# Moving every SBUF tile that TensorE reads to a multiple of 512 bytes

## Chip, cores and metric

One NeuronCore of a Trainium2 chip runs the whole layer as one launch. The metric is the device time of that launch in microseconds (us). The sections on the profile speak of PE (TensorE's matmuls), PEld (its weight loads), DVE (VectorE), ACT (ScalarE), POOL (GpSimd) and SP (the queue that issues nearly all DMAs). In a matmul the *stationary* operand (the weights) is loaded into the array ahead of it, and the *moving* operand is streamed through; both are read from SBUF. SBUF is addressed here in bytes per partition, and "at 352" means 352 bytes past a multiple of 512.

## What is computed

One layer of a hybrid backbone: 1024 latent tokens of width 1024 and 256 context tokens, all fp32.

```
mod = silu(c) @ w_mod + b_mod            # six shift/scale/gate vectors; context has its own
h   = modulate(rms_norm(x), sh1, sc1)    # hc the same for the context
q, k, v, g, f = split(h @ w_in)          # k, v of the context give the first states
y = (sig_r * (ret(q,k,v) readout * silu(g)) @ w_ret_out      # bidirectional retention
   + sig_f * fft2_mix(f) @ w_four_out) @ w_out               # gates: sigmoid(h @ w_bg + b)
x = x + g1 * y
u = conv3(modulate(rms_norm(x), sh2, sc2) @ w_up)            # 2 x 2816 wide
x = x + g2 * (gelu(u_a) * u_v) @ w_down
return rms_norm(x)
```

## The kernel before

Nearly every product is made with three matmuls: each fp32 operand is split into a rounded high part and a remainder (`split`, L96 to L98: ACT casts the high part, DVE subtracts for the low part), both in the type float32r, and hi*hi, hi*lo and lo*hi are summed in PSUM. Three helpers issue them, each in that order of three: `mm3` (L114 to L117; all projections), `chain` (L771 to L775; the up projection) and `step` (L1014 to L1018; the down projection). The up and the down projection use a fast matrix product with seven products of half the size in place of eight.

Counted from the loops, there are 5,268 float32r matmuls with 512 moving columns: 2,496 by `mm3` (the first k/q/v pass `pk` 192, gates `g` 384, `gr` 384 and `gf` 384, Fourier input `f` 192 and output `fo` 192, retention output `re` 384, output projection `wo` 384), 1,848 by `chain` (L774) and 924 by `step` (L1017). Another 1,440 have 256 columns (the context projections `kc` and `vc`, the later `qk` and `v`). The retention itself, the transposes and the small Fourier products are in plain fp32, two passes each, most with 128 columns.

The stages follow each other in the code: norm and first projection (to about 75 us), retention with the projections of the next head pair between its steps (to 550), branch gates and Fourier branch (to 700), retention output and output projection (to 890), transposes and operands of the FFN (to 985), up projection (to 1360), down projection and final norm. The order of instructions on each engine is fixed when the program is built; a planner with estimated durations makes it, so that other work may stand between the matmuls of one loop.

SBUF is filled from both ends. Pools opened with `side="right"` (`wp`, L65: the weights of the projections as `hi`, `lo` and the raw loads; later `fw`: the operands of the up projection) are laid out down from the right end, all others up from the left. A tile's place follows from the sizes of those before it, each rounded up to 32 bytes. The first tile, `ident`, begins at byte 16,512 and the right end is byte 229,344. The pool `const` (L63) holds `ident`, `silrow`, the small vectors and `ones`; after it stand the big tiles of `ap` (the activations `h` hi and lo, later operands of the FFN), then the pool of the stage (`sp` L244, `rp` L353, `zp` and `fp` L597, `bp` and so on). With the sizes in the code:

- all big tiles on the left lie at 352, all on the right at 480, because 229,344 is 480 past a multiple of 512 and the sizes there are multiples of 512;
- in `rp`, the tables `dec` (128 bytes), `lg`, `expc`, `sm` and `smx` stand between bigger tiles, so that the tiles after them (`tab`, `pt`, `on`, `vc`, `kcfb`) lie at 64, while `qT`, `kT`, `kfb`, `qfb`, `ss`, the values and `s0_all` lie at 352;
- in `zp`, `cdft` (516 bytes) and `x64` (80 bytes) push what follows (`wfo`, `X`, `F`) to 480, while `z` and `fourc` lie at 352;
- in the down projection (pool `dp`, L1003) both operands, `oa` and `ob` (and `first`), are on the left at 352.

So `step` has both operands at the same place within 512 bytes, and every other float32r matmul has one operand at 352 and one at 480.

Of the kernel before, what the change touches and what calls it, by code (L numbers as in the profile page):

```python
# [8 lines left out]
F32 = mybir.dt.float32  # L9
# [7 lines left out]
P = 128  # L17
D = 1024
L = 1024
LC = 256  # L20
KD = D // P
# [22 lines left out]
def tile_block(ctx: ExitStack, tc: tile.TileContext, a: dict, out: bass.AP):  # L44
    nc = tc.nc
    V, S, T, G = nc.vector, nc.scalar, nc.tensor, nc.gpsimd
    dma = nc.sync.dma_start

    def tt(out, in0, in1, op):
        V.tensor_tensor(out=out, in0=in0, in1=in1, op=op)  # L50

    def tsc(out, in0, s1, op0, s2=None, op1=None):
        if op1 is None:
            V.tensor_scalar(out=out, in0=in0, scalar1=s1, scalar2=None, op0=op0)
        else:
            V.tensor_scalar(out=out, in0=in0, scalar1=s1, scalar2=s2, op0=op0, op1=op1)
# [3 lines left out]

    ADD, SUB, MUL = ALU.add, ALU.subtract, ALU.mult

    const = ctx.enter_context(tc.tile_pool(name="const", bufs=1))  # L63
    wps = ctx.enter_context(ExitStack())
    wp = wps.enter_context(tc.tile_pool(name="wp", bufs=2, side="right"))  # L65
    ops = ctx.enter_context(ExitStack())
# [17 lines left out]
    mhalf = const.tile([P, 4], F32, name="mhalf")  # L84
    epsc = const.tile([P, 1], F32, name="epsc")
    ycx = silrow[:, :LC]
    ones = const.tile([P, 256], F32, name="ones")
    V.memset(mhalf, -0.5)
    V.memset(epsc, EPS)

# [5 lines left out]
    def split(hi, lo, src):  # L96
        S.copy(hi, src)  # L97
        tt(lo, src, hi.bitcast(F32), SUB)  # L98
# [15 lines left out]
    def mm3(o, l, r, first, last):  # L114
        T.matmul(o, l[0], r[0], start=first, stop=False)  # L115
        T.matmul(o, l[0], r[1], start=False, stop=False)  # L116
        T.matmul(o, l[1], r[0], start=False, stop=last)  # L117
# [4 lines left out]
    def pick(w, *idx):  # L122
        return tuple(t[idx] for t in w)
# [3 lines left out]
    def blk(i, n=P):  # L127
        return slice(i * n, i * n + n)
# [12 lines left out]
    def half():  # L141
        if not halves:
            for i in (0, 1):
                ps = rt(f"half{i}")
                halves.extend((ps[:, :256], ps[:, 256:]))
        halves.append(halves.pop(0))
        return halves[-1]
# [44 lines left out]
    def t2(pool, name, n=512, dt=F32, tag="t2"):  # L192
        return pool.tile([P, 512], dt, tag=tag, bufs=T2[tag], name=name)[:, :n]
# [12 lines left out]
            stt(t1, t1, c, tr, ADD, MUL)  # L206
        stt(dst, t1, 1.0, ti.bitcast(F32), ADD, MUL)

    def rstd_bc(pool, slices, n, name, y=None):
        ps = half()  # L210
        for k in range(KD):
            sq = t2(pool, f"sq{name}{k}", n)
            q = 32 * (k % 4)
            S.activation(sq, slices[k], AF.Square)
            T.matmul(ps[q:q + 32, :n], ones[:, 0:32], sq, start=(k < 4), stop=(k >= 4), tile_position=(0, q))
        part = t2(pool, f"pt{name}", n)
        S.copy(part, ps[:, :n])
        T.matmul(ps[:, :n], ones[:, 128:256], part, start=True, stop=True)
        if y is None:
            y = pool.tile([P, n], F32, name=f"y{name}")  # L220
        u, v = (t2(pool, f"{c}{name}", n) for c in "uv")
        S.activation(y, ps[:, :n], AF.Abs_reciprocal_sqrt, bias=epsc, scale=1.0 / D)
        tsc(v, ps[:, :n], 1.0 / D, MUL, EPS, ADD)
        tt(u, y, y, MUL)
        tt(u, u, v, MUL)
        tsc(u, u, -0.5, MUL, 1.5, ADD)
        tt(y, y, u, MUL)
        return y
# [15 lines left out]
    with tc.tile_pool(name="sp", bufs=1) as sp:  # L244
        xh = [sp.tile([P, KD, 512], F32, name=f"xh{t}") for t in range(2)]
        ccs = sp.tile([P, KD, 2], F32, name="ccs")
        sil = sp.tile([P, KD, 32], F32, name="sil")
        V.memset(sil, 0.0)
        dma(ccs, a["cc"])
        S.activation(sil[:, :, 0:2], ccs, AF.Silu)  # L250
        V.memset(ones[:, 0:128], 1.0)
        V.memset(ones[:, 128:256], 1.0 / 32)
        w0 = [None] * KD

        groups = [(g // 2, blk(g % 2, 256), (2 * g, 2 * g + 1)) for g in range(4)]

        def load_x(g):
            t, c, _ = groups[g]
            for q in range(2):
                dma(xh[t][:, blk(q, 4), c], a["xT"][2 * g + q].rearrange("p (k n) -> p k n", k=4))  # L260

        def x_slices(g):
            t, c, _ = groups[g]
            return [xh[t][:, k, c] for k in range(KD)]

        w0t = [tuple(wp.tile([P, 4, 512], F32R, tag=f"w{n}", name=f"w0{i}{n}") for n in ("hi", "lo")) for i in range(2)]

        def load_w0(q):
            raw = wp.tile([P, 1024], F32, tag="wraw", bufs=3, name=f"w0r{q}")
            dma(raw, a["w_qkv0"][q // 2, q % 2])  # L270
            raw = raw.rearrange("p (k n) -> p k n", k=2)
            for k in range(2):
                w0[2 * q + k] = pick(w0t[q // 2], ALL, 2 * (q % 2) + k)
            ks = slice(2 * (q % 2), 2 * (q % 2) + 2)
            split(w0t[q // 2][0][:, ks], w0t[q // 2][1][:, ks], raw)

        def k_step(k, n, ps):
            mm3(ps, pick(hT[n // 4], ALL, k, blk(n % 4)), w0[k], k == 0, k == KD - 1)

        def h_step(g, k):  # L280
            t, c, _ = groups[g]
            h_slice(xh[t][:, k, c], ys[g], hT[t][0][:, k, c], hT[t][1][:, k, c], k, 0, ONACT[g])

        def k_steps(g, k):
            for n in groups[g][2]:
                k_step(k, n, psk[n])

        def mod(k):
            if k < KD:
                mod_cols(sp, sil, a["wm1"], k)  # L290
                if k % 2 == 0:
                    load_w0(k // 2)

        def rms(g):
            c = groups[g][1]
            return rstd_bc(sp, x_slices(g), c.stop - c.start, f"x{g}")

        psk = [kp.tile([P, 512], F32, name=f"pk{n}") for n in range(6)]
        load_x(0)
        for t, n in ((bmodc, "bmodc"), (norms, "norms"), (sel, "sel")):  # L300
            dma(t, a[n])
        ys = [rms(0)]
        mod(0)
        h_step(0, 0)
        k_steps(0, 0)
        load_x(1)
        ys.append(rms(1))
        mod(1)
        h_step(1, 0)
        k_steps(1, 0)  # L310
        for g in range(2):
            h_step(g, 1)
            k_steps(g, 1)
        load_x(2)
        mod(2)
        ys.append(rms(2))
        h_step(2, 0)
        for g in range(2):
            h_step(g, 2)
            k_steps(g, 2)  # L320
        k_steps(2, 0)
        h_step(2, 1)
        mod(3)
        for k in range(1, KD):
            mod(k + 3)
            if k + 2 < KD:
                h_step(0, k + 2)
                h_step(1, k + 2)
            if k + 1 < KD:
                h_step(2, k + 1)  # L330
            if k == 3:
                load_x(3)
                ys.append(rms(3))
            if k == 4:
                cs = [sp.tile([P, 4, 256], F32, tag="mraw", bufs=8, name=f"cs{i}") for i in range(2)]
                for i in range(2):
                    dma(cs[i], a["ctxT"][:, 4 * i:4 * i + 4, :])
                rstd_bc(sp, [cs[k // 4][:, k % 4, :] for k in range(KD)], LC, "c", ycx)
            if k > 2:
                k_steps(0, k)  # L340
                k_steps(1, k)
            if k >= 4:
                h_step(3, k - 4)
            k_steps(2, k)
        for k in range(KD - 4, KD):
            h_step(3, k)
        psk += [rt(f"pk{n}") for n in (6, 7)]
        for k in range(KD):
            k_steps(3, k)
        wg0 = wload_k(a["w_g"], 0, "wg")  # L350

    T2 = {"t2": 3, "t2b": 3}
    with tc.tile_pool(name="rp", bufs=1) as rp:  # L353
# [4 lines left out]
        hc = [tuple(t4(f"hc{i}{n}", dt=F32R) for n in "hl") for i in range(2)]  # L358
        kcs = t4("kcs", (2, 512))
        s0_all = rp.tile([P, H, P], F32, name="s0_all")  # L360
        dec = rp.tile([P, 32], F32, name="dec")
        lg = rp.tile([P, 32], F32, name="lg")
        expc = rp.tile([P, 6], F32, name="expc")
        ropec = rp.tile([P, NT, 2, 32], F32, name="ropec")
        decm = rp.tile([P, 4, P], F32, name="decm")
        sm = rp.tile([P, 56], F32, name="sm")
        smx = rp.tile([P, 56], F32, name="smx")
        for t, n in ((ropec, "ropec"), (dec, "dec"), (expc, "expc"), (decm, "decm")):
            dma(t, a[n])
        for i in range(2):  # L370
# [148 lines left out]
        for n in range(NT):  # L519
            ps = psk[n].rearrange("p (n c) -> p n c", n=1)  # L520
            t, c = n // 4, slice(n % 4, n % 4 + 1)
# [7 lines left out]
        cs = [ctt[k // 4][:, k % 4, :] for k in range(KD)]  # L529
# [267 lines left out]
    with tc.tile_pool(name="mp", bufs=2, reuse_waits="tile") as mp:  # L797
# [59 lines left out]
        for t in range(2):  # L857
            y = tuple(big(ap if t == 0 else bp, f"y{t}{n}") for n in "hl")
# [50 lines left out]
    with tc.tile_pool(name="ff", bufs=1, reuse_waits="tile") as ff:  # L909
# [76 lines left out]
        for n, i in enumerate(order):  # L986
            cs = up_mm(i)
# [15 lines left out]
    with tc.tile_pool(name="dp", bufs=1, reuse_waits="tile") as dp:  # L1003
# [28 lines left out]
        c = [[dp.tile([P, 512], F32, name=f"c{q}{n}") for n in N4] for q in range(3)]  # L1032
# [202 lines left out]
```

## Time and profile before

| | |
|---|---|
| time, median of 3 runs | 1594.49 us (1592.68 to 1598.33) |
| the profiled execution: its own time | 1593.61 us |
| the profiled execution: span of its instructions | 1591.8 us |
| PE busy, share of the span | 1536.5 us, 97% |
| PEld | 1275.2 us, 80% |
| DVE | 1032.2 us, 65% |
| ACT | 630.0 us, 40% |
| mean granted TensorE clock | 0.986 of full speed |

The busy time of PE is the union of its matmuls, whose ends overlap the starts of the next. A matmul that lasts 390 ns therefore doesn't take 390 ns of the span: what it takes is the distance from its start to the next start. That distance is read from the chain of work that ended last, where consecutive matmuls of one tile are merged into one piece with its length and count, or from the start times in the timeline.

### The profile page before, as it was taken

What the parts mean: (1) busy time and instruction counts of PE and PEld (TensorE: products, weight loads), DVE (VectorE), ACT (ScalarE), POOL (GpSimd) and SP (SyncE); (2) the same over time, 40 slices, a digit from 0 to 9 for tenths busy, and PEclk for the clock granted to TensorE, in tenths of its full rate; (3) what the DMA queues carried; (4) which work ended last, traced back from release to release, by engine and by line L of the source; (5) the groups of instructions that cost most, each with busy time, mean ns of one, the idle gap of its engine ahead of it and who ended that gap; (6) DMA issues with size and microseconds to landing.
All of it is one profiled execution on the core that took longest, in us unless ns stands there. A gap on an engine that the chain in (4) does not pass through costs nothing.

```text
span 1591.8 us, 20417 instructions
## 1 busy us (share of the span) xinstructions
PE 1536.5 (97%) x7806; PEld 1275.2 (80%) x7806; DVE 1032.2 (65%) x1920; ACT 630.0 (40%) x1084; POOL 70.6 (4%) x115
## 2 busy tenths in 40 slices
PE   6999999999999999999999879999999999799996
PEld 3789989898878888888888658888888888678885
DVE  5586848467562552135566688878788787596668
ACT  6554132231322231122354545445445444344443
POOL 0000000000000000000000000110000001000001
PEclk9999999999999999999999889999999999899998
DMA  9235122214442411237385322332222222783324
GB/s 356 98 123 183 60 69 85 73 61 132 128 154 97 154 49 67 80 131 265 120 278 172 120 94 85 120 106 99 99 100 99 99 100 106 270 318 100 94 92 179
DMA packets 76482, 207.45 MB, mean 130 GB/s; under 512 B 9616, under 2 KB 13984, under 8 KB 76384
## 3 DMA queue, kind: packets, MB, share of 16 engines
q1 hardware_dynamic: 70224, 185.96, 34.9%
q0 software_dynamic: 6160, 20.19, 3.4%
q8 instruction: 61, 1.00, 0.3%
q14 instruction: 37, 0.30, 0.1%
HBM read 162.82 MB, written 43.26 MB: 129 GB/s over the span
## 4 chain that ended last, share of the span: by engine, by line
PE 84%; DVE 8%; DMA 5%; ACT 1%; issue 1%; SPq 0%; POOL 0%; DVEq 0%; ACTq 0%; POOLq 0%
PE x L774 16%; PE y L774 8%; PE dx L1017 7%; PE z L774 4%; DMA mt<-wmT 3%; PE dy L1017 2%; PE dz L1017 2%; PE wo L116 2%; PE wo L115 2%; PE gf L115 2%; PE re L117 2%; PE re L115 2%; PE wo L117 2%; PE g L117 2%; PE re L116 2%; PE gf L117 2%
## 5 line engine op out<-in xcount | busy, mean ns | idle before, releaser
L774 PE MATMUL x<-s,wt 128*128 128x512 f32 x528 | 133.0, 397 | 10.1 <-ACT wt L97 10.1
L774 PEld LDWEIGHTS x<-s,wt 128*128 128x128 f32 x528 | 100.0, 190 | 34.3 <-ACT wt L97 10.3
L1017 PE MATMUL dx<-ob,oa 128*128 128x512 f32 x480 | 112.5, 396 | 8.3 <-DVE ob L50 4.8
L1017 PEld LDWEIGHTS dx<-ob,oa 128*128 128x128 f32 x480 | 91.5, 191 | 28.6 <-DVE ob L50 5.5
L50 DVE TENSOR_TENSOR wt<-t,wt 128x512 fp32r<-128x512 f32 x88 | 59.9, 686 | 47.5 <-ACT wt L97 40.0
L179 DVE SCALAR_TENSOR_TENSOR mt<-mt,silrow 128x512 f32<-128x512 f32 x64 | 41.7, 689 | 67.1 <-DMA mt<-wmT 67.1
L50 DVE TENSOR_TENSOR oa<-pr,oa 128x512 fp32r<-128x512 f32 x73 | 50.2, 690 | 52.8 <-ACT oa L97 52.8
L97 ACT CAST oa<-pr 128x512 fp32r<-128x512 f32 x73 | 45.2, 622 | 96.1 <-PE dx L1017 54.2
L774 PE MATMUL x<-a,wb 128*128 128x512 f32 x264 | 67.7, 403 | 2.9 <-DVE acc L50 2.0
L97 ACT CAST wt<-t 128x512 fp32r<-128x512 f32 x88 | 54.4, 623 | 39.3 <-PE x L774 25.6
L774 PE MATMUL z<-a,wb 128*128 128x512 f32 x264 | 70.0, 399 | 0.0
L774 PE MATMUL y<-s,wt 128*128 128x512 f32 x264 | 67.1, 397 | 0.0
L774 PE MATMUL y<-s,wb 128*128 128x512 f32 x264 | 65.2, 395 | 0.0
L774 PE MATMUL x<-a,wt 128*128 128x512 f32 x264 | 65.0, 395 | 0.0
L774 PEld LDWEIGHTS x<-a,wb 128*128 128x128 f32 x264 | 50.9, 194 | 15.8 <-ACT wb L97 3.8
L59 DVE SCALAR_TENSOR_TENSOR t<-ca,convw,t 128x1023 f32<-128x1023 f32 x44 | 56.2, 1278 | 9.6 <-ACT t L952 9.4
L1017 PE MATMUL dy<-ob,oa 128*128 128x512 f32 x264 | 60.8, 390 | 1.2 <-ACT oa L97 1.2
L495 ACT ACTIVATE on<-o,nm,rst 128x128 f32<-128x128 f32 x64 | 24.0, 455 | 94.0 <-DVE nm L59 94.0
L774 PEld LDWEIGHTS z<-a,wb 128*128 128x128 f32 x264 | 50.1, 190 | 11.7 <-ACT wb L97 0.2
L774 PEld LDWEIGHTS y<-s,wt 128*128 128x128 f32 x264 | 50.0, 189 | 11.6
L1017 PEld LDWEIGHTS dy<-ob,oa 128*128 128x128 f32 x264 | 49.4, 188 | 12.1 <-ACT oa L97 1.6
L774 PEld LDWEIGHTS y<-s,wb 128*128 128x128 f32 x264 | 49.7, 188 | 11.6
(946 smaller groups left out, 4096.7 us busy)
## 6 DMA issues: line engine op xcount, KB each, us to landing
pr<-p_d SPq DMA_DIRECT2D x73, 256.0 KB, 2.6
mt<-wmT SPq DMA_DIRECT2D x32, 512.0 KB, 3.9
p_d<-t POOLq DMA_DIRECT2D x44, 256.0 KB, 2.6
d<-w_down SPq DMA_DIRECT2D x44, 256.0 KB, 5.4
p_d<-s POOLq DMA_DIRECT2D x33, 256.0 KB, 3.1
xh<-xT SPq DMA_DIRECT2D x8, 512.0 KB, 7.2
r_d<-rr SPq DMA_DIRECT2D x16, 256.0 KB, 4.0
sr_d<-sr SPq DMA_DIRECT2D x8, 512.0 KB, 4.8
```

The lines of the kernel that those rows point to most:

```text
L50: V.tensor_tensor(out=out, in0=in0, in1=in1, op=op)
L59: V.scalar_tensor_tensor(out=out, in0=in0, scalar=s, in1=in1, op0=op0, op1=op1)
L97: S.copy(hi, src)
L115: T.matmul(o, l[0], r[0], start=first, stop=False)
L116: T.matmul(o, l[0], r[1], start=False, stop=False)
L117: T.matmul(o, l[1], r[0], start=False, stop=last)
L179: V.scalar_tensor_tensor(out=raw[:, c], in0=raw[:, c], scalar=1.0, in1=silrow[:, c], op0=MUL, op1=MUL, accum_out=acc[:, h:h + 1])
L495: S.activation(on[:, n, :], o[:, blk(n)], AF.Identity, bias=nm[:, n:n + 1], scale=rs[:, n:n + 1])
L774: T.matmul(ps, x[:, l, k], y[:, r, k], start=(first and k == 0 and l + r == 0), stop=(k == 3 and l == 1), skip_group_check=True)
L1017: T.matmul(ps[n], x[l][:, blk(n)], y[r], start=(first and l + r == 0), stop=(l == 1), skip_group_check=True)
```

## The change

Two tiles that nothing reads are added and filled with zeros: `edge`, 480 bytes at the right end, and `base`, 40 fp32 words (160 bytes) at the left end of `const`. `ones` moves from `const` to the pool `sp` of the first stage and is handed to `rstd_bc` as an argument. In `rp`, five small tables become slices of one tile `small` of 1,024 bytes. Worked out with the sizes, the left tiles then start at 23,552 (a multiple of 512) and the right end is 228,864 (another one). `wfo`, `X` and `F` come to lie at 128, 128 bytes past `z` as before. The tiles of the first stage behind `ccs` (64 bytes) come to lie at 64. No other instruction is added or taken out.

```diff
+    edge = ctx.enter_context(tc.tile_pool(name="edge", bufs=1, side="right"))
+    V.memset(edge.tile([P, 120], F32, name="edge"), 0.0)
     const = ctx.enter_context(tc.tile_pool(name="const", bufs=1))
+    V.memset(const.tile([P, 40], F32, name="base"), 0.0)
...
-    ones = const.tile([P, 256], F32, name="ones")
...
-    def rstd_bc(pool, slices, n, name, y=None):
+    def rstd_bc(pool, ones, slices, n, name, y=None):
...
         sil = sp.tile([P, KD, 32], F32, name="sil")
+        ones = sp.tile([P, 256], F32, name="ones")
...
         s0_all = rp.tile([P, H, P], F32, name="s0_all")
-        dec = rp.tile([P, 32], F32, name="dec")
-        lg = rp.tile([P, 32], F32, name="lg")
-        expc = rp.tile([P, 6], F32, name="expc")
+        small = rp.tile([P, 2, 128], F32, name="small")
+        dec, lg, expc = small[:, 0, 0:32], small[:, 0, 32:64], small[:, 0, 64:70]
         ropec = rp.tile([P, NT, 2, 32], F32, name="ropec")
         decm = rp.tile([P, 4, P], F32, name="decm")
-        sm = rp.tile([P, 56], F32, name="sm")
-        smx = rp.tile([P, 56], F32, name="smx")
+        sm, smx = small[:, 1, 0:56], small[:, 1, 64:120]
```

## Rows read from the trace of the kernel before

**Rows 1.** The page: busy share of each engine, busy tenths and granted clock by slice.

```profile
PE 1536.5 (97%) x7806; PEld 1275.2 (80%) x7806; DVE 1032.2 (65%) x1920; ACT 630.0 (40%) x1084; POOL 70.6 (4%) x115
...
PEclk9999999999999999999999889999999999899998
```

**Rows 2.** Busy time by stage: stretch, its length, each engine's busy us, clock.

```profile
75.00:550.00 475.00, 471.98 (x3060) 422.65 (x3059) 288.32 (x749) 146.90 (x258) 17.31 (x16) 1.00 0.33 108
...
640.00:800.00 160.00, 160.00 (x690) 129.69 (x690) 63.02 (x71) 42.41 (x52) 0.55 (x1) 1.00 0.46 155
...
890.00:985.00 95.00, 81.90 (x337) 65.40 (x338) 73.85 (x121) 51.36 (x90) 2.79 (x3) 0.88 0.30 98
985.00:1360.00 375.00, 375.00 (x1616) 304.11 (x1615) 303.69 (x397) 178.28 (x264) 37.69 (x70) 1.00 0.31 105
```

**Rows 3.** PE's longest waits: who waited for whom, total us, times, longest.

```profile
PE x L774 <- ACT wt L97: 10.1, 1, 10.1
PE half L215 <- ACT sqx L214: 6.2, 1, 6.2
```

**Rows 4.** Chain that ended last, up projection: start, length in us, piece and count.

```profile
1014.84 5.57 PE x L774 x24
...
1065.03 5.58 PE x L774 x24
```

**Rows 5.** The same chain in the down projection.

```profile
1487.85 29.92 PE dx L1017 x132
1517.77 29.92 PE dz L1017 x132
```

**Rows 6.** Timeline of PE, first fo matmul and the gf after 24 of them.

```profile
642.85 0.39 PE L115 MATMUL fo<-zh,wfo0hi 128*128 128x512 f32 x1
...
648.44 0.40 PE L115 MATMUL gf<-h0h,wbf6hi 128*128 128x512 f32 x1
```

**Rows 7.** The chain from 700 us: its longest single matmuls, in order of time.

```profile
713.43 0.24 PE fo L115
715.05 0.24 PE fo L116
716.68 0.24 PE re L117
718.31 0.24 PE re L115
719.93 0.24 PE re L116
```

**Rows 8.** Timeline of PE, 256 columns: two stretches, first and last row of each.

```profile
109.08 0.28 PE L115 MATMUL kc<-wkc0hi,hc0h 128*128 128x256 f32 x1
...
111.96 0.28 PE L115 MATMUL kc<-wkc0hi,hc0h 128*128 128x256 f32 x1
...
186.03 0.28 PE L115 MATMUL v<-wv1hi,h0h 128*128 128x256 f32 x1
...
187.10 0.28 PE L115 MATMUL v<-wv1hi,h0h 128*128 128x256 f32 x1
```

**Rows 9.** Timeline of PE, plain fp32 in two passes with 256 columns, and what follows.

```profile
565.69 1.02 PE L656 MATMUL zc<-fourc,X 128*128 128x256 f32 x4
566.55 0.38 PE L659 MATMUL zc<-fourc,X 128*128 128x128 f32 x2
```

**Rows 10.** The chain at 153 us: plain fp32 with 128 columns.

```profile
153.64 1.79 PE kv L455 x16
```

**Rows 11.** The page, costliest groups: instruction, count, busy us, mean ns of one.

```profile
L50 DVE TENSOR_TENSOR wt<-t,wt 128x512 fp32r<-128x512 f32 x88 | 59.9, 686 | 47.5 <-ACT wt L97 40.0
...
L50 DVE TENSOR_TENSOR oa<-pr,oa 128x512 fp32r<-128x512 f32 x73 | 50.2, 690 | 52.8 <-ACT oa L97 52.8
```

**Rows 12.** Timelines at the start and of the small tables: DVE, PE and SP's queue.

```profile
1.17 0.17 DVE L251 MEMSET ones<- 128x128 f32 x1
...
6.23 2.30 PE L215 MATMUL half<-sqx,ones 128*32 128x256 f32 x9 [6.23 <-ACT sqx L214]
...
77.91 0.91 SPq L371 DMA_DIRECT2D ctt<-ctxT  x2
...
97.37 0.42 DVE L50 TENSOR_TENSOR hc1l<-ctt,hc1h 128x256 fp32r<-128x256 f32 x1
...
110.76 0.28 PE L117 MATMUL kc<-wkc0hi,hc1l 128*128 128x256 f32 x1
```

**Rows 13.** Tiles dec and expc: time from a DMA's issue to its landing.

```profile
DMA to landing us min/median/max: 2.4/2.4/2.4
...
DMA to landing us min/median/max: 2.7/2.7/2.7
```

More of the change, by code (lines that the diff above doesn't have):

```diff
@@ L295, in rms @@
             c = groups[g][1]
-            return rstd_bc(sp, x_slices(g), c.stop - c.start, f"x{g}")
+            return rstd_bc(sp, ones, x_slices(g), c.stop - c.start, f"x{g}")
         psk = [kp.tile([P, 512], F32, name=f"pk{n}") for n in range(6)]
@@ L337, in tile_block @@
                     dma(cs[i], a["ctxT"][:, 4 * i:4 * i + 4, :])
-                rstd_bc(sp, [cs[k // 4][:, k % 4, :] for k in range(KD)], LC, "c", ycx)
+                rstd_bc(sp, ones, [cs[k // 4][:, k % 4, :] for k in range(KD)], LC, "c", ycx)
             if k > 2:
```

## Prediction

> **What bounds the kernel now.** I read the page first: PE is busy for 97% of the span at a granted clock of 0.9 or more in nearly every slice [rows 1]. The table by stage says where that holds without a gap: from 75 to 550 us, from 640 to 800 and from 985 to 1360 PE is busy for all or nearly all of the stretch at clock 1.00, which is the upper level, 2.4 GHz, while DVE has room (304 of 375 us in the up projection, its fullest stage). Only around 890 to 985 does something else set the pace [rows 2]. PE's longest wait of the whole run is 10.1 us [rows 3]. So the time is the number of matmuls times the distance between their starts, and a change of that distance shows nearly whole in the result. That makes the distance the thing to read.
>
> At 2.4 GHz and one column per cycle, 512 columns take 512 / 2.4 = 213.3 ns. No float32r matmul here reaches that. In the up projection 24 take 5.57 or 5.58 us, 232.3 ns each [rows 4]; in the down projection 132 take 29.92 us, 226.7 ns each, in two stretches alike [rows 5]. Same shape, same type, same clock, and the order hi*hi, hi*lo, lo*hi is the same; the difference of 5.7 ns is 2.4%.
>
> What differs is where the operands lie. In the down projection both lie at 352; in the up projection one is at 352 on the left and one at 480 on the right of SBUF. Distance alone isn't it: `fo` reads `z` and `wfo`, both on the left and within 60 KB of each other, one at 352 and one at 480, and 24 of its matmuls take 648.44 - 642.85 = 5.59 us, 232.9 ns each [rows 6]. Nor does it matter which operand is at 480: the first pass and `wo` have the moving one there, the other loops the stationary one, and the longest single matmuls return alike in `fo` and `re`, every 1.63 us, which is every seventh matmul [rows 7]. They take 0.24 us, the rest less. Such a beat is what two interleaved reads make that get into each other's way at a changing moment: the moving columns of one matmul and the weights of the next. Where the places agree there is no beat, only a steady 13.3 ns over the 213.3.
>
> **The change part by part.**
>
> *Places.* After it, both operands of every float32r matmul lie at 0 but for `fo`, whose weights stay 128 bytes off their moving operand. So the relation that only `step` has now holds for all 512-column matmuls but 924 that have it already and 192 of `fo`: 5,268 - 924 - 192 = 4,152. If they come to the 226.7 ns of rows 5, that is 4,152 x (232.4 - 226.7) = 23.7 us less. The trace shows no float32r matmul at a multiple of 512, so whether the absolute place counts too has to be bounded: at worst nothing is gained by it (226.7), at best the steady 13.3 ns goes as well. The nearest row for the best is plain fp32 with 256 columns in two passes, the same 512 array cycles, at 352: four in 0.86 us, 215 ns each [rows 9]. So the array can follow at 215; I take 226.7, since it is measured with this type and differs by nothing but the absolute place, and keep 215 for the range.
>
> *256 columns.* These 1,440 need 106.7 ns at the same rate, and take 2.88 us / 24 = 120.0 ns in one stretch and 1.07 us / 9 = 118.9 in another, at the same places [rows 8]. None has both operands at one place. The nearest row is the steady excess of rows 5, 13.3 ns per matmul, which gives 120.0: 1,440 x 1.0 = 1.4 us more. The other end is what plain fp32 with 128 columns shows, 1.79 us for 16, 111.9 ns each [rows 10], at which a new set of weights can evidently follow the last: 1,440 x 7.1 = 10.2 us less. I take the first.
>
> *Plain fp32.* The retention's matmuls run at 111.9 ns with operands at 352, 64 and 128 mixed, so place doesn't show there; 0, and at most some 700 x 2 ns = 1.4 us.
>
> *Other engines.* DVE's subtraction takes 686 ns where its operands are at 480 and 352 and 690 where all are at 352 [rows 11]: elementwise work doesn't care, 0.
>
> *Two memsets.* They come first on DVE. `ones`, 128 columns, takes 0.17 us and is through by 1.5; PE's first matmul starts at 6.23 after ACT's squares of the first load [rows 12]. Hidden; 0.3 us if that cover were gone.
>
> *The shared tile.* Five tables in one tile bring no operation. Should loads and writes of different slices be held apart by waits, `dec` and `expc` would queue on SP with the `ctt` load issued behind them at 77.91, by up to 2.4 + 2.7 = 5.1 us [rows 13]. What needs `ctt` is the context's `hc`, whose last part DVE begins at 97.37 and PE first reads at 110.76, after the gate projection: a cover of some 13 us [rows 12]. 0, and at most 5.1 us.
>
> *`ones` in `sp`.* Written by the same two memsets, read last by the same matmuls as the square sums of that pool, so the pool is held no longer; 0.
>
> *What doesn't follow.* Between 890 and 985 us PE has 13 us of idle time that the matmuls don't set, and some matmuls run at the half clock after waits; I take 0.8 us off the gain for that. In the up projection DVE would be busy for 304 of some 366 us, still not the bound.
>
> Sum, against the profiled execution's 1593.6 us: -23.7 + 1.4 + 0.8 = -21.5, so 1572.1. That execution lies 0.9 us under the median of the runs, so 1573 for the median.
>
> **The rivals.**
>
> *A, as above: the relative place counts.* 1573; with the ends for 256 columns and the shared tile 1561 to 1580.
>
> *B, the absolute place counts as well.* A read that starts off a boundary takes in one block more than it needs; with 32 columns of four bytes, 128 bytes, that block would cost 32 / 2.4 = 13.3 ns, just the steady excess of rows 5. At 215 ns: 4,344 x 17.4 = 75.6 us from those at 232.4, 924 x 11.7 = 10.8 from `step`, 10.2 from the 256 columns; less some 8 us where DVE and loads then come late in the retention's stage: 89 us less, 1505. For it: the exact 13.3. Against it: a strict block more would make 120.0 the floor for 256 columns, and rows 8 show 118.9. The Trainium skill (TensorE: Matmul & The Clock Gate, "Wait — 56ns, not 53.3ns?") gives 215.7 ns from start to start for warm back-to-back matmuls of 512 columns in general, without a word on places; by that figure B's sum would be 3 us smaller. No float32r matmul of this trace comes near it.
>
> *C, neither counts.* Then the 5.7 ns are the down projection's for another reason (its output tiles change every three matmuls, its operands are single 4 KB tiles) and nothing moves: 1594.5. Against it: `wo` and the first pass change their output tile as often, and run with the rest. The Trainium skill (the same page, "Step-by-step: what each phase is for") holds that the two operands have independent read ports and that loading the next weights takes no read bandwidth from the running matmul. By that rule the place of one against the other can't count, and the result is C's. The trace speaks against it with 226.7 beside 232.3 and 232.9 [rows 4 to 6], though it can't show ports.
>
> *D, the fixed relation is a bad one for other loops.* The beat of rows 7 goes through good and bad moments; a fixed place could lock a loop into the bad one, 0.24 us at each matmul rather than at each seventh. `step` reads its operands from tiles it shares with nobody; with twelve matmuls on one output and weights far off the lock may fall elsewhere. At 241 ns: 4,152 x 8.6 = 35.7 us more, 1630. It decides from the point where the mean of the up projection exceeds 232.4 ns. For it: loops of one shape with the same places settle at different rates, 120.0 and 118.9 ns [rows 8]. Against it: both stretches of rows 5 and all three accumulators of the down projection are in the good one.
>
> **How the numbers follow.** A 0.48, B 0.27, C 0.14, D 0.11. Faster by over 0.3% (what a measurement of this kernel can tell from no change) is A and B, 0.75; within is C, 0.14; slower is D, 0.11. The range leaves out D, the lower part of B and some of C: 1502 to 1596.
>
> **What would show it.** Under A the pieces of the up projection shrink from 5.57 to 5.44 us for 24, single matmuls of 0.24 us vanish from the chain, `fo` stays at 232 to 233 as a control, and the down projection stays at 29.92 for 132. Under B the down projection shrinks too, to about 28.4, and `fo` moves. Under C all pieces are as they were. A down projection that got slower would refute the comparison on which all this rests. The prediction is wrong in its base if the planner orders the matmuls differently because of the new tiles and new waits over 5 us stand in PE's list.

## The result, and the profile after

The changed kernel takes 1574.99 us (median) beside 1593.59 for the kernel before; the ratio on record is 0.987, with a 95% interval of 0.9835 to 0.9906. One of its four executions took 3915.77 us, for a reason that isn't known; it counts as slow and is left out of the ratio (the median of the other three is 1574.07). In a second measurement the ratio was 0.9878 (0.9863 to 0.9893). The profiled execution took 1574.07 us, its span is 1572.3 us; before it was 1591.8. The forecast was 1573, case A.

The page of the kernel after, with its busy shares and the granted clock by slice, answers to [rows 1]:

```profile
PE 1517.1 (96%) x7806; PEld 1273.7 (81%) x7806; DVE 1031.6 (66%) x1922; ACT 630.1 (40%) x1084; POOL 70.6 (4%) x115
PEclk9999999999999999999999989999999999899998
```

PE has 19.4 us less busy time with the same 7,806 matmuls, and they come in the same order; the mean granted clock is 0.985, beside 0.986 before. DVE has two instructions more, the memsets. So no work was taken away. The table by stage (stretch, length, busy us of PE, PEld, DVE, ACT and POOL, clock, DMA share, GB/s), to be read beside [rows 2], shows where the gain lies: in stretches where PE has no gap.

```profile
638.70:796.80 158.10, 158.10 (x696) 130.35 (x695) 64.61 (x75) 44.72 (x56) 1.11 (x2) 1.00 0.47 163
974.70:1340.60 365.90, 365.90 (x1616) 302.99 (x1615) 303.27 (x397) 178.26 (x264) 37.70 (x70) 1.00 0.30 108
```

The first stretch holds 696 matmuls in 158.1 us, where before 690 took 160.0. The up projection does its 1,616 matmuls in 365.9 us where it took 375.0, with PE busy without a gap in both. The chain of work that ended last (start, length in us, piece and its number of matmuls) says what one of them costs. Two pieces of the up projection and two of the down projection, against [rows 4, 5]:

```profile
1003.77 5.44 PE x L775 x24
1014.65 5.44 PE x L775 x24
...
1468.32 29.92 PE dx L1018 x132
1498.24 29.92 PE dz L1018 x132
```

5.44 / 24 = 226.7 ns where it was 232.3; and the down projection, whose operands lay at one place before, is unchanged to the hundredth. The control hasn't moved either. In the timeline of PE, the first `fo` and the `gf` after 24 of them [rows 6]:

```profile
639.60 0.40 PE L117 MATMUL fo<-zh,wfo0hi 128*128 128x512 f32 x1
...
645.19 0.39 PE L117 MATMUL gf<-h0h,wbf6hi 128*128 128x512 f32 x1
```

That is 5.59 us for 24, as before. And 256 columns, first row and the row 24 matmuls later [rows 8]:

```profile
108.09 0.28 PE L117 MATMUL kc<-wkc0hi,hc0h 128*128 128x256 f32 x1
...
110.97 0.28 PE L117 MATMUL kc<-wkc0hi,hc0h 128*128 128x256 f32 x1
```

2.88 / 24 = 120.0 ns. Averaged over the whole trace (start to next start within a loop) the changed 512-column matmuls went from 232.4 to 227.0 ns, the 256-column ones from 119.1 to 119.8, `fo` stayed at 232.7.

**Adding it up.** Since the order of the matmuls is the same, the n-th matmul of one trace can be set against the n-th of the other. The lead of the kernel after grows by 0.57 us per hundred matmuls in `re`, `wo` and the up projection (5.7 ns each), by some 0.3 in the stretch where `gf` alternates with the unimproved `fo`, and by nothing in the down projection. It is 0.8 us at matmul 1,000; then 1.6 us are lost between matmuls 1,000 and 1,100; it is 2.5 us at matmul 3,600, 10.4 at the start of the up projection, 19.4 at its end and 19.5 at the end of the kernel. With the means above: 4,152 x 5.4 = 22.4 us less, 1,440 x 0.7 = 1.0 more, 1.6 more: 19.8, against 19.5 of the spans. Not every loop pays out: over the 192 matmuls of `pk`, in the first 86 us, the lead grows by 0.04 us, since PE has gaps there.

**The 1.6 us.** They are a wait. PE's list of waits (who waited for whom, total us, times, longest) for the scores `sc` in before, in after and in the kernel of the second experiment below (`e2_right_256`), which has the same tiles on the left as after:

```profile
PE sc L472 <- DVE ss L59: 1.3, 2, 0.9
```

```profile
PE sc L473 <- DVE ss L59: 2.7, 3, 1.5
```

```profile
PE sc L473 <- DVE ss L59: 0.5, 1, 0.5
```

`ss` is late on DVE because DVE stood idle some 20 us earlier for a load, `mt`. The timeline of DVE (start, length, instruction; in brackets the idle time ahead of it and what ended it), again before, after and `e2_right_256`:

```profile
148.23 0.69 DVE L179 SCALAR_TENSOR_TENSOR mt<-mt,silrow 128x512 f32<-128x512 f32 x1 [3.48 <-DMA mt<-wmT]
```

```profile
149.10 0.69 DVE L181 SCALAR_TENSOR_TENSOR mt<-mt,silrow 128x512 f32<-128x512 f32 x1 [5.23 <-DMA mt<-wmT]
```

```profile
146.70 0.69 DVE L181 SCALAR_TENSOR_TENSOR mt<-mt,silrow 128x512 f32<-128x512 f32 x1 [3.48 <-DMA mt<-wmT]
```

DVE waited 1.75 us longer than before, although the load was issued 0.9 us earlier, and from there to the scores its instructions start 0.9 us later than in before, where PE's start 0.8 us earlier. The trace's list for this tile gives the time from the DMA's issue to its landing as (min/median/max) 3.5/3.9/4.4 in before, 3.4/4.0/6.2 in after and 3.4/3.8/4.4 in `e2_right_256`: one `mt` load of after took 1.8 us longer. Kernels with the same tiles have it or don't, so it isn't the shared tile; the kernel of the first experiment, which has no shared tile at all, has a longest landing of 6.4 us and the longest single wait of `sc` is 1.8 us there. It is no property of one kernel either: `e4_best` and `e7_best` below are the same program, and its longest landing was 4.4 us in one execution and 5.8 in the other, its longest single wait of `sc` 1.1 and 2.0 us. What made those transfers slow isn't shown.

### The profile page after: what moved, and what is told of

The parts are those of the page before. It is cut to its first block, busy times and chain, and to the rows that moved or that the text cites. A ratio compares the mean times of both kernels' runs of the same rounds, so it can differ in the third digit from the quotient of the medians.

```text
span 1572.3 us, 20419 instructions
## 1 busy us (share of the span) xinstructions
PE 1517.1 (96%) x7806; PEld 1273.7 (81%) x7806; DVE 1031.6 (66%) x1922; ACT 630.1 (40%) x1084; POOL 70.6 (4%) x115
## 4 chain that ended last, share of the span: by engine, by line
PE 86%; DVE 8%; DMA 3%; ACT 1%; issue 1%; SPq 0%; POOL 0%; DVEq 0%; ACTq 0%
PE x L775 15%; PE y L775 8%; PE dx L1018 7%; PE dy L1018 4%; PE z L775 4%; DMA mt<-wmT 2%; DVE ss L59 2%; PE dz L1018 2%; PE re L117 2%; PE gf L117 2%; PE wo L118 2%; PE g L119 2%; PE wo L117 2%; PE re L119 2%; PE wo L119 2%; PE gf L119 2%
## 5 line engine op out<-in xcount | busy, mean ns | idle before, releaser
L775 PEld LDWEIGHTS y<-s,wt 128*128 128x128 f32 x264 | 49.8, 189 | 10.4
```

The costliest lines, as they stand in the source:

```text
L775: T.matmul(ps, x[:, l, k], y[:, r, k], start=(first and k == 0 and l + r == 0), stop=(k == 3 and l == 1), skip_group_check=True)
```

## Experiments

**Both at 352.** Before, with 128 bytes at the right end and nothing else: no `base`, no moved `ones`, no shared tile. Left and right then both lie at 352.

```diff
+    edge = ctx.enter_context(tc.tile_pool(name="edge", bufs=1, side="right"))
+    V.memset(edge.tile([P, 32], F32, name="edge"), 0.0)
     const = ctx.enter_context(tc.tile_pool(name="const", bufs=1))
```

> The kernel before with one edit: 128 bytes of padding at the right end of SBUF, so that the right tiles lie at 352 like the left ones; no base pad, no moved ones, no shared tile. Theory A (the place of one operand against the other counts): the 512-column matmuls come to 226.7 ns as in the changed kernel, the time is that of the changed kernel, 1575 us within 4 us. Theory B (a multiple of 512 itself counts): the 512-column matmuls stay above 226.7 and the time lies between 1580 and 1594.

1571.44 us, ratio 0.9869 (0.985 to 0.9888). The chain in the up projection:

```profile
1006.92 5.44 PE x L776 x24
1017.80 5.44 PE x L776 x24
```

The mean distance over the trace is 227.0 ns for 512 columns, 119.9 for 256, 232.7 for `fo`: after's values. So two lines are enough for the whole gain, and a multiple of 512 has no part in it. B falls, and the rest of the diff isn't needed.

**The right side at 256.** After, with `edge` at 184 instead of 120 words; left operands at 0, right ones at 256.

```diff
-    V.memset(edge.tile([P, 120], F32, name="edge"), 0.0)
+    V.memset(edge.tile([P, 184], F32, name="edge"), 0.0)
```

> The changed kernel with 256 bytes more of padding at the right end: left tiles at 0, right tiles at 256. Theory A with agreement as the good case: up projection back to a beat, 232 ns or more per 512-column matmul, time 1590 or more; the down projection (both on the left) stays at 226.7. Theory B: both are multiples of 256, time near 1575. Open by either: whether 256 apart is worse or better than 128 apart (232.4).

1571.8 us, ratio 0.9875 (0.9859 to 0.9891), and the pieces of the up projection again take 5.44 us for 24 in the chain:

```profile
1001.17 5.44 PE x L775 x24
1012.05 5.44 PE x L775 x24
```

My expectation missed. Operands 256 bytes apart are as good as operands at one place; "the same place within 512 bytes" was too narrow.

**A map of places.** No part of the layer is computed: a stream of 96 matmuls, then 256 streams of 24 float32r matmuls with 512 columns in the layer's order of hi and lo, moving operand at 0, 32, ... 480 and stationary operand likewise.

```diff
+    for m in range(16):
+        for s in range(16):
+            stream(f"p{ABC[m]}{ABC[s]}", 24, 8 * m, 8 * s)
```

> No part of the layer is computed: a stream of 24 float32r matmuls with 512 columns for each of 16 places of the moving operand and 16 of the stationary operand, in steps of 32 bytes within 512. Theory A: the distance between starts depends on the difference of the two places alone, 226.7 ns on the diagonal and 232 to 233 where they are 128 bytes apart. Theory B: it depends on each place by itself, lowest at 0 and 0. Rival, the read ports don't disturb each other: one value everywhere.

The chain, one line per stream; the second letter is the place of the moving operand in steps of 32 bytes (a is 0), the third that of the stationary one:

```profile
126.20 5.48 PE pbb L42 x24
131.68 5.59 PE pbc L42 x24
137.27 5.60 PE pbd L42 x24
142.87 5.61 PE pbe L42 x24
148.48 5.60 PE pbf L42 x24
154.08 5.60 PE pbg L42 x24
159.69 5.51 PE pbh L42 x24
165.19 5.59 PE pbi L42 x24
170.79 5.45 PE pbj L42 x24
...
1028.39 5.45 PE pld L42 x24
...
1072.94 5.45 PE pll L42 x24
```

From `pbb` the stationary operand moves away in steps of 32 bytes, and at `pbj`, 256 bytes on, the fast piece is back. `pld` (352 and 96) and `pll` (352 and 352) are as fast. Without the first matmuls of each stream, where the change of places is still in the distances, the mean distance of 16 streams each is:

| stationary minus moving, modulo 256 | 0 | 32 | 64 | 96 | 128 | 160 | 192 | 224 |
|---|---|---|---|---|---|---|---|---|
| ns | 226.7 | 233.4 | 233.5 | 234.3 | 233.4 | 233.5 | 228.9 | 233.3 |

The same eight numbers come at 256 to 480, to a tenth, and the 16 streams of one difference agree within 0.3 ns in nearly every case (some of 128 show 232.4, the number of the layer). So for 512 columns, in steps of 32 bytes, the difference of the two addresses modulo 256 sets the distance (and its sign counts: 64 and 192 aren't alike), and nothing else about the places tried does. Only 0 is fast, and 192 nearly so; the other six lie within 1 ns of each other.

**Other forms.** The same streams (none of the layer) with float32r and 256 columns, bfloat16 and 512, plain fp32 and 256 in two passes, each at 16 places of the stationary operand, and float32r at offsets below 32 bytes.

```diff
+            stream(f"q{ABC[m]}{ABC[s]}", 36, 8 * m, 8 * s, 256)
+            stream(f"h{ABC[m]}{ABC[s]}", 24, 16 * m, 16 * s, 512, mvb, stb)
+        stream(f"f{ABC[s]}", 12, 0, 8 * s, 256, mvf, stf)
+        stream(f"m{ABC[s]}", 24, s, 0)
```

> No part of the layer is computed: streams of matmuls as in the map, for 256 columns of float32r, 512 columns of bfloat16, 256 columns of plain fp32, and places that differ by 4 to 32 bytes. Theory A: 256 columns 120.0 ns where the places agree, 118 to 120 elsewhere; bfloat16 and plain fp32 need less than the full rate of four bytes a column and show no dependence on place (bfloat16 near 216 ns). If the reads share something by address whatever the type, bfloat16 depends on it too.

The chain: bfloat16 at differences 32 and 128 (`hab`, `hae`), plain fp32 at 32 (`fb`; 24 are 12 matmuls of two passes), two of the small offsets, the moving operand 20 and 28 bytes on (`mf`, `mh`), and float32r with 256 columns at 64 and at 320, which is 64 modulo 256 (`qac`, `qak`):

```profile
176.39 5.18 PE hab L51 x24
...
191.93 5.18 PE hae L51 x24
```

```profile
342.15 5.18 PE fb L51 x24
```

```profile
497.73 5.76 PE mf L51 x24
...
509.09 5.44 PE mh L51 x24
```

```profile
44.66 3.86 PE qac L51 x34
...
77.48 4.24 PE qak L51 x36
```

bfloat16 and plain fp32 take 5.18 / 24 = 215.8 ns at every place tried: of these three types the place counts for float32r alone. At 20 bytes float32r is at its worst, 240.0 ns; at 28 it is as fast as at 0 (226.7). With 256 columns the means are 120.0 at difference 0, 118.3 (32), 113.3 or 117.8 (64), 117.3 or 120.0 (96), 117.8 (192), and 116.7 to 120.1 at the others: here 0, best for 512 columns, is among the worst. At 64 and 96 two levels appear, at equal differences modulo 256 and modulo 512 alike, so for 256 columns the difference alone doesn't fix the distance. In the width run below six streams at 64, each after plain fp32, all took 117.8; when 113.3 comes is not settled.

The Trainium skill (TensorE: Matmul & The Clock Gate, "Step-by-step: what each phase is for") says that loading the next weights takes no read bandwidth from the running matmul. The 215.8 ns at every place agree with that for bfloat16 and plain fp32. For float32r the place of one operand against the other changes the distance, 226.7 against 233 to 234 ns, which two reads that don't touch each other wouldn't give; the measurement decides, though no run shows the reads themselves.

**The right side at 96.** After, with the place that the map has as the worst.

```diff
-    V.memset(edge.tile([P, 120], F32, name="edge"), 0.0)
+    V.memset(edge.tile([P, 96], F32, name="edge"), 0.0)
```

> The changed kernel with the right end 96 bytes above a multiple of 512 in place of 0 (the pad there is 384 bytes). By the map, 96 bytes apart is the worst place, 234.3 ns: 3,576 matmuls with their weights 96 bytes ahead take 7.6 ns more than now, 576 with the moving operand on the right (160 by the map) 6.8 more, 31 us together. Theory A with the map's sizes: 1603 us, 0.7% slower than the kernel before. Rival, the gain came with the changed kernel's other edits or its order of work: time near 1575.

1597.43 us, ratio 1.0034 (1.0021 to 1.0047): slower than before. The chain:

```profile
1066.06 5.62 PE x L775 x24
1094.17 5.62 PE x L775 x24
```

5.62 / 24 = 234.2 ns with the stationary operand 96 ahead; the loops with the moving one 96 ahead (difference 160) take 233.4 on average. The map says 234.3 and 233.5, so it holds in the layer. The size in my expectation was off: 31 us over after, where the two ratios (1.0034 and 0.9878) give some 25. Set against before's own distances (232.4, and 232.6 in the loops with the moving operand on the right), 3,576 x 1.8 + 576 x 0.8 + 1,440 x 0.8 ns (256 columns, 119.9 against 119.1) are 8.1 us more. The medians differ by 7.0 us; the ratio gives 5.4, its interval 3.3 to 7.5. What the rest is stays open.

**Without the right pad.** After less `edge`: `base`, the shared tile and the moved `ones` stay, left operands at 0, right ones at 480.

```diff
-    edge = ctx.enter_context(tc.tile_pool(name="edge", bufs=1, side="right"))
-    V.memset(edge.tile([P, 120], F32, name="edge"), 0.0)
```

> The changed kernel without the pad at the right end: left tiles at 0, right tiles at 480 (224 within 256); base pad, moved ones and shared tile stay. Theory A with the map: 233.3 ns for 3,576 matmuls (0.9 more than the kernel before) and 233.4 for 576, 118.3 for the 1,440 of 256 columns (0.8 less): 1,590 + 3.2 + 0.5 - 1.2, about 1593, within 0.3% of the kernel before. Theory B, the left tiles at a multiple of 512 are worth something by themselves: between 1575 and 1588.

1594.16 us, ratio 1.0012 (1.0002 to 1.0022). The chain:

```profile
1011.47 5.60 PE x L773 x24
1022.67 5.60 PE x L773 x24
```

5.60 / 24 = 233.3 ns, the map's value for a difference of 224, and the whole gain is gone. The big tiles of the left side lie at multiples of 512 here, and it brings nothing. With the first experiment this separates the diff: the relation between the two ends of SBUF is what counts, and the rest has no time of its own that these runs show.

**A version made from the map.** The remaining two groups are put at their best places: `fo`'s weights at `z`'s place (96 words of padding in `zp`) and the 256-column operands so that the stationary one is 64 bytes ahead; 128 bytes at the right end, no `base`.

```diff
-    V.memset(edge.tile([P, 120], F32, name="edge"), 0.0)
+    V.memset(edge.tile([P, 32], F32, name="edge"), 0.0)
...
-    V.memset(const.tile([P, 40], F32, name="base"), 0.0)
...
+        off = 48 if name in ("wkc", "wvc", "wqk", "wv") else 0
+        hi, lo = (... .tile([P, 2112 if off else 2048], F32R, ...)[:, off:off + 2048] ...)
...
+        zp.tile([P, 96], F32, name="zpad")
```

> The changed kernel with wfo brought to its moving operand's place (384 bytes more in zp), and the weights of the 256-column matmuls 192 bytes further on, so that the stationary operand lies 64 bytes ahead by the map; pads reduced to 128 bytes at the right end to make room. fo falls from 232.7 to 226.7 ns, 1.1 us less. The 256-column matmuls fall from 120.0 to 117.8 or 113.3 ns (the streams showed both for this place), 3.2 to 9.6 us less. Theory A with the map: 1561 to 1568 us. If the 256-column matmuls are not on the path that sets the end there, near 1571.

1568.16 us, ratio 0.985 (0.9827 to 0.9873). `fo` now runs with the rest: no single matmul stands out in its stretch of the chain, where all have 0.23 us, and its mean is 227 ns. 256 columns average 117.8 ns in `kc` and `vc`, 116.9 in `qk` and 116.1 in `v`, the latter two a mixture of distances near 113 and near 118. The time is at the upper end of what I had expected. To set it against after on one chip, both were run again side by side:

> The changed kernel once more, beside the next one on the same chip: ratio to the kernel before 0.987 to 0.989.

> The kernel with wfo at its moving operand's place and the 256-column weights 192 bytes further on, once more. By the distances read from its trace, 1,440 x (119.8 - 116.7) + 192 x 6 ns = 5.6 us less than the changed kernel. Theory A: 0.3 to 0.4% under it in this call. If the 256-column matmuls' gain is lost in waits of the retention on DVE, 0.1% or nothing.

After took 1573.5 us (0.9878 of before, 0.9863 to 0.9893), this version 1567.46 (0.9847, 0.9827 to 0.9867). The medians lie 6.0 us apart, the ratios 0.0031, some 4.9 us; worked out from the distances it is 192 x 5.7 + 1,440 x 3.1 = 5.6 us. The intervals touch at their edges, so that it beats before is clear, that it beats after by 0.3% likely.

**Width.** What are the 10.9 ns that float32r at its best place still has over bfloat16 (226.7 - 215.8)? If they were the time in which weights are read, fewer weight columns or weights used again should shorten them. Streams alone, none of the layer: 32 to 128 weight columns, 64 to 512 moving columns, and one set of weights throughout.

```diff
+            stream(f"w{ABC[i]}{ABC[d]}", 36, 0, 8 * d, 512, wide=wide)
+            stream(f"n{ABC[i]}{ABC[d]}", 36, 0, 8 * d, 64 * i + 64)
+        stream(f"one{ABC[d]}", 36, 0, 8 * d, one=True)
```

> No part of the layer is computed: streams of float32r matmuls with 32, 64, 96 and 128 weight columns and 512 moving columns, with 64 to 512 moving columns and 128 weight columns, with one and the same weights throughout, and repeated streams of 256 columns after plain fp32. Where the remaining 10.9 ns above bfloat16's 215.8 are the weight read's share, they shrink with the number of weight columns, to about 3 at 32; and the rise from 64 to 512 moving columns is 0.417 ns per column with a fixed part of 13.3. If they are the type's own fixed cost, the width doesn't matter. If the 113.3 and 117.8 ns of 256 columns depend on what ran before, the repeats differ among themselves.

The chain, all at the upper clock: 32 and 128 weight columns (`waa`, `wda`), 320 and 512 moving columns (`nea`, `nha`), one set of weights (`onea`), all at difference 0:

```profile
36.55 7.88 PE waa L47 x34
...
133.02 8.17 PE wda L47 x36
...
259.17 5.28 PE nea L47 x36
...
334.62 8.16 PE nha L47 x36
...
367.79 8.19 PE onea L47 x36
```

5.28 / 36 = 146.7 and 8.16 / 36 = 226.7 ns: the 192 columns between them take 80.0 ns, 1 / 2.4 each, and both leave 13.3 ns over their columns, as do 256 (120.0). 384 columns leave 13.6, 448 leave 16.1. So at equal places the excess hardly grows with the columns. It is no fixed cost of the type either: at other places 256 columns leave 6.7 (113.3 ns), and 448 leave 13.3 at a difference of 192 (200.0 ns), while 320 take 146.7 at all four differences. With 64 and 192 columns the distance stays at 111.7 ns.

Narrower weights are slower at difference 0, 230.0 to 231.6 ns, although 32 columns are loaded in 109 ns and 128 in 188 (the LDWEIGHTS of `waa` and `wda`); at a difference of 64 it is the other way round (96 columns 228.3, 128 columns 233.3). So reading time in proportion to the weights is ruled out at difference 0. One set of weights throughout doesn't change the distance (226.8 without the first of the stream), but that stream still loads it ahead of each matmul, 36 times, so no run shows what leaving out the load would give. What the 13.3 ns are stays open.

## Why the prediction was right

*The base.* Counting matmuls and distances was the right way to the time: the order on PE is the same, no new wait over 5 us stands in its list, and 19.8 us by distances and one wait meet the 19.5 of the spans. But "only around 890 to 985" was too narrow a reading of the table: PE is busy for 62.9 of the first 75 us and for 208.1 of the last 232, so that the 192 matmuls of `pk`, 1.1 us of the sum, brought next to nothing; the last stretch holds few matmuls that change.

*The main term* was sized at 4,152 x 5.7 = 23.7 us and measured 22.4. The 5.7 is the steady difference (232.4 less 226.7; from the 232.3 of the text it would be 5.6); averaged over each loop, with the starts of the loops, it is 5.4.

*256 columns* were taken to go to the 13.3 ns over their columns, 1.4 us more; they went to 119.8 on average, 1.0 more. The bound of 10.2 us less was out of reach at this place, and the streams of 256 columns show that some of it lies at another (64), with 113 to 118 ns.

*The 0.8 us for the stretch around 890 to 985* were not needed: over the 400 matmuls before the up projection's unbroken stretch, from 874 us, the lead grows by 2.4 us, 0.6 per hundred like elsewhere. That is in part chance: 0.7 us of it come from seven transposes at 890 us whose starts lay 213 to 268 ns apart before and 109 to 165 after.

*The shared tile, the memsets, `ones`*: nothing is seen of them; without any of these three the first experiment is as fast. *Plain fp32*: 215.8 ns at every place. *DVE* was put at 0, and its two groups in the page say so, beside [rows 11]:

```profile
L50 DVE TENSOR_TENSOR wt<-t,wt 128x512 fp32r<-128x512 f32 x88 | 59.8, 685 | 43.2 <-ACT wt L99 43.2
...
L50 DVE TENSOR_TENSOR oa<-pr,oa 128x512 fp32r<-128x512 f32 x73 | 50.1, 688 | 52.8 <-ACT oa L99 52.8
```

*What the sum left out* is the 1.6 us of `sc`. I had weighed waits that the new tile could cause; the one that came was a load that landed later in this execution. PE has little slack in the retention, and terms of 1 to 2 us there can't be forecast from one trace. That the forecast came within 2 us is thus partly luck: 1.3 us too much in the main term and this wait pulled one way, 0.4 and 0.8 us too much on the other side.

*The signs.* Pieces of 5.44 us, `fo` at 232 to 233, the down projection at 29.92: as announced. The single matmuls of 0.24 us are gone from `re` and remain, every 1.63 us, in `fo`. The chain after 706 us, beside [rows 7]:

```profile
706.61 0.24 PE fo L118
708.24 0.24 PE fo L119
709.86 0.24 PE fo L117
```

*The rivals.* B rested on 13.3 ns being just 32 columns, read in excess because 352 is no boundary. The 13.3 is there at every one of 16 absolute places where both operands agree, 0 included, and in the changed kernel at 0, so the coincidence meant nothing. (The 3 us that 215.7 in place of 215 takes off B's gain are 3.7: 5,268 x 0.7 ns.) C is refuted by the layer itself, through `e5_no_edge` against after: one pad less, the same code, 1594.16 against 1573.5 us on one chip. D had a true core: some fixed relations are worse than before's, and 96 makes the kernel 5 to 7 us slower than before. But its price was too high: in steps of 32 bytes, which is what tiles are rounded to, the worst mean is 234.3 ns, not 241, so that D could have cost some 8 us rather than 36. A value near 241 appears only at an offset of 20 bytes. And at equal places, the relation that the change makes, the lock is good in every loop tried, so D doesn't hold for this change.

*Where a step was wrong.* "What differs is where the operands lie" was right, but places were compared within 512 bytes, and for 512 columns the period is 256. It made no difference to this sum, since 352 and 480 are 128 apart under either, and 0 and 0 agree under both; it made the expectation of the second experiment miss. Two places only, 352 and 480, stood in the trace of before, and from two places no period can be read. That two interleaved reads get into each other's way at a changing moment, the reason that I gave for the beat, fits the dependence on the difference but was not tested by itself.

## What to carry over

Where PE is busy without a gap, read the distance between the starts of its matmuls, loop by loop, and compare loops of the same shape and type: a difference of 2% between two of them is a lead that no list of waits shows. For float32r with 512 columns, place both operands at the same address modulo 256; when pools grow from both ends of SBUF, one small tile at one end does it, and a later change of any tile size can undo it. Measure a map of places apart from the kernel before choosing one, since the best place for 512 columns is not the best for 256.

## What the runs showed of the hardware that I had not expected

- The distance of float32r matmuls of 512 columns depends on (stationary - moving) modulo 256 bytes and, over 16 x 16 places in steps of 32 bytes, on no absolute place: 226.7 ns at 0, 228.9 at 192, 233.3 to 234.3 at the other multiples of 32 (some streams at 128: 232.4); 240.0 with the moving operand 20 bytes on, 226.7 with it 28 bytes on.
- bfloat16 (512 columns) and plain fp32 (256 columns, two passes) take 215.8 ns at every place. float32r with 512 columns is 10.9 ns slower per matmul at its best place. At equal places its excess over the columns is 13.3 ns for 256, 320 and 512 columns alike (384: 13.6, 448: 16.1); 320 columns take 146.7 ns at all four differences tried.
- 256 columns of float32r take from 113.3 to 120.1 ns by place, with two levels at differences of 64 (113.3 and 117.8) and 96 (117.3 and 120.0).
- At equal places weights of 32 to 96 columns make a float32r matmul slower (230.0 to 231.6 ns against 226.7), though 32 columns are loaded in 109 ns and 128 in 188; loading the same weights each time makes it no faster (226.8).
- The slowest load of the tile `mt` between 130 and 165 us took from 4.4 to 6.4 us to land, by execution; where it was over 5.5, PE's longest wait for the scores some 20 us afterwards was 1.2 to 2.0 us, elsewhere 0.5 to 1.1.
